# Hybrid attention and HGRN2 block: value tiles turned in 32x32 blocks at eviction instead of by TensorE transposes

## The chip, the cores and the metric

One Trainium2 chip, of which the kernel uses one core. The metric is the device time of one execution in microseconds (us); where several executions are timed, their median. Inputs and output are float32, batch 1, 1024 tokens, model width 1024.

The engines are named as the profile names them: PE (TensorE matmul; PEld is its weight load), DVE (VectorE), ACT (ScalarE), POOL (GpSimd) and SP (SyncE, which here issues most of the DMAs). SBUF is the on-chip memory of 128 partitions, PSUM the memory that PE writes to, DRAM the memory off the core.

## The reference

One encoder block. Only the parts that touch "values" matter here:

```python
h = layer_norm(x, ln_in_g, ln_in_b)
proj = h @ w_in[l]                       # 1024 x 11776
aq, ak, av, hq, hf_fwd, hf_bwd, hi, hg, ga, gh = jnp.split(proj, split_idx, axis=-1)
att = dilated_attention(aq, ak, av, slopes)      # 3 groups (dilation 1, 4, 16) x 8 heads x 64
rec = hgrn2(hq, hf_fwd, hf_bwd, hi, hg, ...)     # 8 heads, 128 keys x 128 values
merged = sigmoid(ga) * (att @ w_att_up[l]) + sigmoid(gh) * (rec @ w_hgrn_up[l])
h = layer_norm(ALPHA * h + merged @ w_o[l], ...)
h = layer_norm(ALPHA * h + (silu(gate) * up) @ w_ffn_out[l], ...)

# attention inside one residue stream
o = jnp.einsum('nbhqk,nbkhd->nbqhd', p, vb) / l
# gated linear recurrence, chunk by chunk
o_intra = jnp.einsum('bhnij,bhnjv->bhniv', a, v)
u = jnp.einsum('bhnck,bhncv->bhnkv', k * jnp.exp(cum_last - cum), v)
```

The values are `av` (attention, 3 groups of 512 columns) and `hi` (recurrence, 1024 columns). In each of the three einsums the values are summed over tokens, so on PE they have to stand with tokens on the partitions. The projection leaves them the other way round, with its output columns on the partitions.

## The kernel before

The program has three phases. Phase 1 (to about 1173 us of the span) makes the whole projection and, woven into it, the attention and the recurrence; phase 2 the merge and `w_o`; phase 3 the feed-forward part. The change touches phase 1 alone.

**The projection, the main stream.** `stream` (L657) makes the 92 column tiles of `w_in`, 128 columns each, four at a time (two groups of two tiles). A pair of tiles is a 2x2 block product made with seven products instead of eight (`ORDER`, L628). Each product is 12 matmuls of 128x512 into one PSUM bank (`pj`): four slices of the inner dimension, and three float32r matmuls per slice (L273 to L275: high by high, high by low, low by high). Weights come in blocks of 128x512 (tile `wa`, issued by SP at L252), are split into `w_hi` (ACT, L215) and `w_lo` (POOL, L225), and three products lie between that split and its use. The sums of weight blocks that the scheme needs are made by DVE and POOL (L697 to L702).

**The evictions.** After four of the seven products a half tile (128 columns by 512 tokens) is complete, and an eviction function takes it out of the bank: `plain` (L564) for attention q, k, v and the recurrence's v; `tanhs` and `silu2` for the others. Where the scheme has a kept partial result (`add`), `plain` adds it in DVE (L573); where it has none (one half tile in four), ACT copies (L571). The half goes to a buffer `evh`, of which there are three, and from there SP stores it to a scratch tensor in DRAM (L574): `hg{h}v` for the recurrence's head h, `at{j}v{g}` for head pair j and group g. All scratch tensors are 128 columns (partitions) by 1024 tokens. For attention groups 1 and 2 the tokens are permuted on the way (`order_src`, `order_dst`), so that the tokens of one residue stream stand side by side. A bank that an eviction empties is written again three products later.

**The units, woven in.** When a unit's columns are stored, it begins: eight units of `hgrn_side` (one head each) and four pairs of `att_far` (groups 1 and 2) and `att_near` (group 0). They are generators; each `yield` gives the number of products of the main stream that come before the next piece. Within what the yields allow, a scheduler orders each engine's instructions. A unit fetches its tensors from scratch (`fetch`, L773) into slots of SBUF. Values then are turned by `turned` (L784): eight PE transposes of 128x128 (L790, into two banks `sd`) and two ACT copies of 128x512 back to SBUF (L791). A recurrence head does that once (tile `hv`), a pair of attention heads three times (tile `v` of group 1, `vt` of group 2, `v` of group 0). Group 2 needs its tokens in yet another order first, which POOL makes with two copies (L899).

What comes next in a unit: in the recurrence the transposes of the keys (L1197), their copies (L1198) and the state products (L1213), which use `hv`; in `att_far` the transposes of the probabilities (L911, L919) and the products with the values (L942 to L951); in `att_near` L1072 and L1088.

Of the kernel before, what the change touches and what calls it, by code (L numbers as in the profile page):

```python
# [10 lines left out]
F32 = mybir.dt.float32  # L11
# [9 lines left out]
T = 1024  # L21
KT = D // 128
HALF = 512
# [8 lines left out]
HQ, HF, HB, HI, HG = 4608, 5632, 6656, 7680, 8704  # L32
# [47 lines left out]
class Block:  # L80
    evac_ahead = 1000

    def __init__(self, ctx, tc, x, ln_in_g, ln_in_b, w_in, hgrn_lb, hgrn_norm_g, w_att_up, w_hgrn_up,
                 w_o, ln1_g, ln1_b, w_ffn_in, w_ffn_out, ln2_g, ln2_b, tabs, out, dbg=None):
        self.tc, self.nc, self.ctx = tc, tc.nc, ctx
        self.x = x[0]
        self.ln = {"in": (ln_in_g, ln_in_b), "1": (ln1_g[0], ln1_b[0]), "2": (ln2_g[0], ln2_b[0])}
        self.w_in, self.lbw, self.ng = w_in[0], hgrn_lb, hgrn_norm_g[0]
        self.wa, self.wr, self.wo = w_att_up[0], w_hgrn_up[0], w_o[0]
        self.wfi, self.wfo, self.tabs, self.out = w_ffn_in[0], w_ffn_out[0], tabs, out[0]  # L90
        self.dbg = dbg or {}
# [12 lines left out]
        def scratch(name, n):  # L104
            if name in self.dbg:
                return [self.dbg[name][i] for i in range(n)]
            return [dram.tile([128, 1024], F32, name=f"{name}{i}") for i in range(n)]

        self.att_d = scratch("att", 4)
        self.rec_d = scratch("rec", 8)  # L110
        self.tg_d = scratch("tg", 16)
        self.n1_d = scratch("n1", 8)
        self.ahs_d = scratch("ahs", 8)
        self.hg_d = [{n: dram.tile([128, T], F32, name=f"hg{h}{n}") for n in ("t0", "t1", "q", "v", "g")}
                     for h in range(8)]
        self.at_d = [{(k, g): dram.tile([128, T], F32, name=f"at{j}{k}{g}") for k in "qkv" for g in range(3)}
                     for j in range(4)]
        self.w_d = [dram.tile([32, 128], F32, name=f"wd{j}") for j in range(4)]
        self.td = [dram.tile([128, 4, HALF], F32, name=f"td{i}") for i in range(3)]
        self.gd = {p: dram.tile([128, NF // 2, HALF], F32, name=f"gd{p}") for p in range(1, 8)}  # L120
        self.consts()
# [442 lines left out]
    def plain(self, dst, g=0, kind="v"):  # L564
# [10 lines left out]

        return evac

    def tanhs(self, dst):
        nc = self.nc

        def evac(l, ps, add):
            t = self.evh()
            if add is not None:
                self.left(nc.vector.tensor_add(t, add, ps))  # L584
            nc.scalar.activation(t, ps if add is None else t, AF.Tanh, scale=0.5)
            nc.sync.dma_start(dst[:, HALF * l:HALF * (l + 1)], t)

        return evac
# [16 lines left out]
    def tiles(self):  # L605


        out, units = [], []
        for i in range(4):
            for h in (2 * i, 2 * i + 1):  # L610
                d = self.hg_d[h]
                for n, col, f in (("t0", HF, self.tanhs), ("t1", HB, self.tanhs), ("q", HQ, self.silu2),
                                  ("v", HI, self.plain), ("g", HG, self.silu2)):
                    out.append((col + 128 * h, f(d[n], len(out) % 2) if n in "qg" else f(d[n])))
                units.append((len(out), h, self.hgrn_pre, self.hgrn_side))
            for g in (1, 2, 0):
                for kind, off in (("q", AQ), ("k", AK), ("v", AV)):
                    out.append((off + 512 * g + 128 * i, self.plain(self.at_d[i][kind, g], g, kind)))
                if g == 2:
                    units.append((len(out), i, self.att_pre, self.att_far))  # L620
            units.append((len(out), i, self.near_pre, self.att_near))
        for i in range(16):
            out.append((GA + 128 * i, self.tanhs(self.tg_d[i])))
        return out, units
# [156 lines left out]
            self.nc.sync.dma_start(t, src)  # L781
        return t

    def turned(self, dst, cols):  # L784

        nc = self.nc
        for b in range(2):
            ps = self.ps_sd()
            for k in range(4):
                nc.tensor.transpose(ps[:, 128 * k:128 * (k + 1)], cols(4 * b + k), self.ident)  # L790
            nc.scalar.copy(dst[:, 4 * b:4 * b + 4, :], ps.rearrange("p (k d) -> p k d", k=4))  # L791
        return dst

    def att_small(self, n, w=8):
        return self.smt.tile([128, 2, w], F32, name=n, tag=n, bufs=1)
# [30 lines left out]
    def att_far(self, j, qk):  # L826


        nc, ident, HD, d = self.nc, self.ident, self.HD, self.at_d[j]
# [3 lines left out]
        q, k = qk  # L833
# [19 lines left out]
        for r in range(4):  # L853
# [5 lines left out]
            for hd, ps in enumerate(pss):  # L859
                for h in range(2):  # L860
                    s, c = slice(192 * h, 192 * h + 192), 2 * r + h
                    self.ttr(P1(r, hd)[:, s], ps[:, s], bias[hd][:, s], M1[:, hd, c:c + 1])
            if r % 2:
                yield 2
        v1, v2 = self.fetch(0, "v1", d["v", 1], True), self.fetch(1, "v2", d["v", 2])
        k2 = k2.rearrange("p (h r i m) -> p r i h m", h=2, r=4, i=4)
        for b in range(2):
            pss = [self.ps_sd().rearrange("p (t c) -> p t c", t=4) for _ in range(2)]
            for jj in range(4):
                r, h = divmod(4 * b + jj, 2)  # L870
# [13 lines left out]
        for r in range(4):  # L884
            for hd in range(2):
                s1, _, s2, _ = self.FAR[2 * r + hd]
                for h in range(2):
                    c = 2 * r + h
# [5 lines left out]
                        nc.scalar.activation(v, v, AF.Exp, bias=N12[:, hd, c:c + 1], scale=QSCALE,  # L894
                                             accum_out=l[:, hd, c:c + 1])
        nc.vector.tensor_add(L12, L12, LB)
        V2 = self.slot(6, "vt2", (8, 128))
        for h in range(2):
            nc.gpsimd.tensor_copy(V2.rearrange("p k (i h m) -> p (k i) h m", i=2, h=2)[:, :, h],  # L899
                                  v2[:, HALF * h:HALF * (h + 1)].rearrange("p (k m) -> p k m", m=32))  # L900
        yield 2
        V1 = self.turned(v1.rearrange("p (k d) -> p k d", k=8), lambda kt: v1[:, 128 * kt:128 * kt + 128])
        self.turned(V2, lambda kt: V2[:, kt, :])
        yield 2


        def turn1(r):
            for hd in range(2):
# [74 lines left out]
    def att_near(self, j, pre):  # L983
# [3 lines left out]
        OL, N12, L12 = self.far  # L987
        q, k, bias = pre
        M0, N0, L0 = (self.att_small(n) for n in ("M0", "N0", "L0"))
        v = self.fetch(0, "v0", d["v", 0])  # L990
        yield 1
        P = []

# [7 lines left out]
        for b in range(4):  # L1001
# [272 lines left out]

    def hgrn_side(self, h, st):
        nc = self.nc
        v = self.fetch(5, "hv", self.hg_d[h]["v"])
        st["fa"] = self.slot(6, "fa")
        steps = [self.hgrn_dir(h, d, st) for d in range(2)]
        for _ in range(2):  # L1280
            for z in steps:
                next(z)
                yield 1
        vT = self.turned(v.rearrange("p (k d) -> p k d", k=8), lambda c: v[:, 128 * c:128 * c + 128])
        k0 = self.hgrn_keys(st, 0)
        for z in steps:
            next(z)
# [755 lines left out]
```

## Time and profile before

| | us |
|---|---|
| three timed executions | 2032.02, 2033.93, 2038.81 (median 2033.93) |
| the profiled execution, its own time | 2036.54 |
| its span in the profile | 2034.7 |
| granted TensorE clock, mean | 0.998 |
| busy: PE, DVE, POOL, ACT | 2003.3, 1312.7, 1013.0, 957.6 |
| DMA: bytes moved, share of 16 engines (SP's queue) | 301 MB, 42.8% |

The profile is one execution. Its page has the busy time of each engine, slices of the span, the DMA queues, the chain that ended last, and groups of equal instructions with their releasers. Beside it, answers of the trace are used: a stretch of the timeline, the instructions of one line or one tile, busy times by windows of 50 us, and who waited for whom. Matmuls overlap in their pipeline, so what one costs is read from start to start and not from its duration. A column of three numbers such as 270/272/273 is shortest/median/longest in ns.

### The profile page before, as it was taken

The page shows a single profiled execution, that of the slowest core. Times are in us where ns is not written, and L with a number is a line of the kernel's source. Part 1 is how long each engine was busy: PE and PEld are TensorE (multiplying, and loading weights), DVE is VectorE, ACT ScalarE, POOL GpSimd, SP SyncE. Part 2 cuts the span into 40 slices and gives each one's busy share as a digit, 9 for nine tenths or more (in the row PEclk, how much of TensorE's full clock was granted, in tenths as well). Part 3 has the DMA queues.
Part 4 walks back from the last instruction along what each step waited for, and adds up shares of the span by engine and source line. Part 5 has one row for each costly group of instructions (what it writes and reads, how often), then busy time and mean ns, then how long its engine had stood idle before and what let it go on. Part 6 is the DMA issues. An engine that isn't in the chain of part 4 may idle for free. (4 is left out here: it accounts for less than half of the span.)

```text
span 2034.7 us, 30875 instructions
## 1 busy us (share of the span) xinstructions
PE 2003.3 (98%) x10942; PEld 1661.3 (82%) x10942; DVE 1312.7 (65%) x2065; ACT 957.6 (47%) x1976; POOL 1013.0 (50%) x882
## 2 busy tenths in 40 slices
PE   7999999999999999999999999999999999999998
PEld 5788888788888888888888888888788888888886
DVE  7876544875458843778444226557776776767788
ACT  6654455554556535655365423244433333344541
POOL 6556653576436663466645662243765665630000
PEclk9999999999999999999999999999999999999999
DMA  5444543345343453443535377444444443347533
GB/s 160 129 132 138 170 127 109 138 149 162 122 150 126 133 173 107 141 136 124 178 99 177 125 255 235 147 145 139 139 136 140 135 140 130 128 169 288 166 97 126
DMA packets 275900, 301.16 MB, mean 148 GB/s; under 512 B 14433, under 2 KB 207906, under 8 KB 275746
## 3 DMA queue, kind: packets, MB, share of 16 engines
q1 hardware_dynamic: 269248, 277.93, 42.8%
q10 hardware_dynamic: 6498, 21.27, 2.7%
q8 instruction: 86, 1.41, 0.3%
q14 instruction: 68, 0.56, 0.1%
HBM read 204.96 MB, written 94.18 MB: 147 GB/s over the span
## 5 line engine op out<-in xcount | busy, mean ns | idle before, releaser
L225 POOL TENSOR_TENSOR w_lo<-wa,w_hi 128x512 fp32r<-128x512 f32 x272 | 363.8, 1347 | 286.8 <-ACT w_hi L215 253.4
L215 ACT CAST w_hi<-wa 128x512 fp32r<-128x512 f32 x272 | 168.5, 620 | 249.7 <-PE pj L274 143.9
L225 POOL TENSOR_TENSOR w_lo<-wsum,w_hi 128x512 fp32r<-128x512 f32 x88 | 127.9, 1464 | 111.1 <-PE sd L275 60.7
L225 POOL TENSOR_TENSOR w_lo<-f_raw,w_hi 128x512 fp32r<-128x512 f32 x66 | 100.9, 1536 | 51.8 <-ACT w_hi L215 50.7
L211 POOL TENSOR_TENSOR mv<-mv,mhalf 128x1 f32<-128x1 f32 x16 | 12.7, 792 | 221.7 <-DVE mv L210 221.6
L215 ACT CAST w_hi<-wsum 128x512 fp32r<-128x512 f32 x88 | 54.6, 621 | 116.7 <-PE sd L274 108.8
L215 ACT CAST gwsum<-a_raw 128x512 fp32r<-128x512 f32 (+1 forms) x78 | 48.2, 618 | 112.2 <-PE pj L274 53.6
L273 PE MATMUL pj<-xt1hi,w_hi 128*128 128x512 f32 x252 | 99.8, 396 | 0.0
L275 PE MATMUL pj<-xt1hi,w_lo 128*128 128x512 f32 x252 | 98.7, 392 | 0.0
L274 PE MATMUL pj<-xt1lo,w_hi 128*128 128x512 f32 x252 | 98.4, 391 | 0.0
L699 POOL TENSOR_TENSOR wa<-wa,wa 128x512 f32<-128x512 f32 x46 | 66.6, 1449 | 55.2 <-DVE wa L698 52.1
L225 POOL TENSOR_TENSOR w_lo<-ws,w_hi 128x512 fp32r<-128x512 f32 x46 | 63.7, 1387 | 57.5 <-ACT w_hi L215 47.3
L584 DVE TENSOR_TENSOR evh<-wkeep,pj 128x512 f32<-128x512 f32 x45 | 30.8, 684 | 93.4 <-PE pj L275 50.6
L573 DVE TENSOR_TENSOR evh<-wkeep,pj 128x512 f32<-128x512 f32 x66 | 57.9, 884 | 37.4 <-PE pj L275 28.7
L727 ACT COPY wkeep<-pj 128x512 f32<-128x512 f32 x136 | 79.5, 586 | 0.1
L273 PE MATMUL pj<-xt2hi,w_hi 128*128 128x512 f32 x192 | 76.5, 399 | 2.0 <-ACT w_hi L215 2.0
L275 PE MATMUL pj<-xt2hi,w_lo 128*128 128x512 f32 x192 | 76.5, 399 | 1.0 <-POOL w_lo L225 0.8
L274 PE MATMUL pj<-xt2lo,w_hi 128*128 128x512 f32 x192 | 76.3, 397 | 0.6 <-DVE xt2lo L405 0.6
L225 DVE TENSOR_TENSOR gwkeep<-a_raw,gwsum 128x512 fp32r<-128x512 f32 (+1 forms) x78 | 53.1, 680 | 36.1 <-ACT gwsum L215 33.2
L273 PE MATMUL pj<-xt4hi,w_hi 128*128 128x512 f32 x192 | 76.3, 397 | 0.0
L273 PE MATMUL pj<-xb11hi,w_hi 128*128 128x512 f32 x192 | 75.9, 398 | 0.3 <-DVE evh L600 0.3
L274 PE MATMUL pj<-xb11lo,w_hi 128*128 128x512 f32 x192 | 75.7, 395 | 0.0
(448 smaller groups left out, 6564.9 us busy)
## 6 DMA issues: line engine op xcount, KB each, us to landing
wa<-in_w_in_dram SPq DMA_DIRECT2D x184, 256.0 KB, 3.5
f_raw<-in_w_ffn_in_dram SPq DMA_DIRECT2D x44, 512.0 KB, 4.1
a_raw<-gd SPq DMA_DIRECT2D x30, 512.0 KB, 3.7
gd<-fc SPq DMA_DIRECT2D x44, 256.0 KB, 2.0
gd<-fs SPq DMA_DIRECT2D x33, 256.0 KB, 2.1
tg<-evh SPq DMA_DIRECT2D x32, 256.0 KB, 2.5
tg<-tg SPq DMA_DIRECT2D x16, 512.0 KB, 5.8
y<-ahs SPq DMA_DIRECT2D x16, 512.0 KB, 6.6
```

The lines of the kernel that those rows point to most:

```text
L211: nc.gpsimd.tensor_tensor(mv[:, 2:3], mv[:, 2:3], self.mhalf[:, 0:1], OP.pow)
L215: ins = nc.scalar.copy(hi, src) if eng_hi == "act" else nc.vector.tensor_copy(hi, src)
L225: ins = e.tensor_sub(lo, src, hi.bitcast(F32))
L273: nc.tensor.matmul(ps, whi, xhi, start=first, stop=False, **kw)
L274: nc.tensor.matmul(ps, whi, xlo, start=False, stop=False, **kw)
L275: self.product = nc.tensor.matmul(ps, wlo, xhi, start=False, stop=last, **kw).ins.name
L573: self.left(nc.vector.tensor_tensor(o, self.order_src(add, g, kind), s, OP.add))
L584: self.left(nc.vector.tensor_add(t, add, ps))
L699: nc.gpsimd.tensor_sub(a["a21"], a["a22"], a["a11"])
L727: nc.scalar.copy(t, ps)
```

## The change

Values are turned where they leave the projection, and never on PE.

- The eviction of a value half is now `rows`. It adds the kept part in DVE where there is one (plain order, no permutation), then one DVE instruction, `transpose`, turns each 32x32 block of the 128x512 half in place; without a kept part the transpose reads the bank itself. A block then has tokens on its 32 partitions, but the blocks still stand where they stood. The store puts them in their places: four DMAs, one for each group of 32 columns, write 32 x 16 pieces of 32 floats (128 bytes) into a scratch tensor that has 1024 rows (tokens) of 128 floats.
- The units fetch the values as rows with `fetch_rows`: tokens come to the partitions by the address pattern of the load. Group 0 and the recurrence take one DMA, group 1 two, group 2 eight (32 partitions each); the order by residue streams, which `order_src` and POOL's copies made before, lies in those patterns.
- `turned` is gone, with its transposes and copies, and POOL's copies for group 2. The yields are unchanged. `plain` stays for q and k.

```diff
-        self.hg_d = [{n: dram.tile([128, T], F32, name=f"hg{h}{n}") for n in ("t0", "t1", "q", "v", "g")}
+        self.hg_d = [{n: dram.tile([128, T], F32, name=f"hg{h}{n}") for n in ("t0", "t1", "q", "g")}
...
+        for h in range(8):
+            self.hg_d[h]["v"] = dram.tile([T, 128], F32, name=f"hg{h}v")
+        for j in range(4):
+            self.at_d[j].update({("v", g): dram.tile([T, 128], F32, name=f"at{j}v{g}") for g in range(3)})
...
+    def rows(self, dst):
+        nc = self.nc
+
+        def evac(l, ps, add):
+            t = self.evh()
+            if add is not None:
+                self.left(nc.vector.tensor_add(t, add, ps))
+            nc.vector.transpose(t, ps if add is None else t)
+            for a in range(4):
+                s = slice(32 * a, 32 * a + 32)
+                nc.sync.dma_start(dst[HALF * l:HALF * (l + 1), s].rearrange("(b i) j -> i b j", i=32),
+                                  t[s, :].rearrange("i (b j) -> i b j", j=32))
+
+        return evac
...
-                                  ("v", HI, self.plain), ("g", HG, self.silu2)):
+                                  ("v", HI, self.rows), ("g", HG, self.silu2)):
...
-                    out.append((off + 512 * g + 128 * i, self.plain(self.at_d[i][kind, g], g, kind)))
+                    dst = self.at_d[i][kind, g]
+                    out.append((off + 512 * g + 128 * i, self.rows(dst) if kind == "v" else self.plain(dst, g, kind)))
...
-    def turned(self, dst, cols):
-
-        nc = self.nc
-        for b in range(2):
-            ps = self.ps_sd()
-            for k in range(4):
-                nc.tensor.transpose(ps[:, 128 * k:128 * (k + 1)], cols(4 * b + k), self.ident)
-            nc.scalar.copy(dst[:, 4 * b:4 * b + 4, :], ps.rearrange("p (k d) -> p k d", k=4))
-        return dst
+    def fetch_rows(self, n, name, src, g=0):
+
+        t = self.slot(n, name, (8, 128))
+        if g == 0:
+            self.nc.sync.dma_start(t, src.rearrange("(k p) d -> p k d", p=128))
+        elif g == 1:
+            z = src.rearrange("(h x r) d -> h x r d", h=2, r=4)
+            for h in range(2):
+                self.nc.sync.dma_start(t.rearrange("p (r h) d -> p r h d", h=2)[:, :, h], z[h])
+        else:
+            z = src.rearrange("(h m e i r) d -> i h e m r d", h=2, e=2, i=2, r=4)
+            for i in range(2):
+                for h in range(2):
+                    for e in range(2):
+                        p = 64 * i + 32 * h
+                        self.nc.sync.dma_start(t.rearrange("p (r e) d -> p r e d", e=2)[p:p + 32, :, e], z[i, h, e])
+        return t
...
-        v1, v2 = self.fetch(0, "v1", d["v", 1], True), self.fetch(1, "v2", d["v", 2])
+        V1, V2 = self.fetch_rows(0, "v1", d["v", 1], 1), self.fetch_rows(1, "v2", d["v", 2], 2)
...
-        V2 = self.slot(6, "vt2", (8, 128))
-        for h in range(2):
-            nc.gpsimd.tensor_copy(V2.rearrange("p k (i h m) -> p (k i) h m", i=2, h=2)[:, :, h],
-                                  v2[:, HALF * h:HALF * (h + 1)].rearrange("p (k m) -> p k m", m=32))
         yield 2
-        V1 = self.turned(v1.rearrange("p (k d) -> p k d", k=8), lambda kt: v1[:, 128 * kt:128 * kt + 128])
-        self.turned(V2, lambda kt: V2[:, kt, :])
         yield 2
...
-        v = self.fetch(0, "v0", d["v", 0])
+        V = self.fetch_rows(0, "v0", d["v", 0])
...
-        V = self.turned(v.rearrange("p (k d) -> p k d", k=8), lambda kt: v[:, 128 * kt:128 * kt + 128])
...
-        v = self.fetch(5, "hv", self.hg_d[h]["v"])
+        vT = self.fetch_rows(5, "hv", self.hg_d[h]["v"])
...
-        vT = self.turned(v.rearrange("p (k d) -> p k d", k=8), lambda c: v[:, 128 * c:128 * c + 128])
```

The order in which the instructions stand shows what becomes of three places. Line numbers of the change are some lines higher than those of before (L573 is L588, L273 is L277, L911 is L932, L697 is L717).

PE, first pair of attention heads, before: the transposes of the values (L790) between two products of the main stream (`pj<-...`).

```order
L275 MATMUL pj<-xb21hi,w_lo 128x512
L790 MATMUL sd<-tabs_sb,v_2778 128x128 x8
L273 MATMUL pj<-xt2hi,w_hi 128x512
L274 MATMUL pj<-xt2lo,w_hi 128x512
L275 MATMUL pj<-xt2hi,w_lo 128x512
L273 MATMUL pj<-xt2hi,w_hi 128x512
L790 MATMUL sd<-tabs_sb,vt_2860 128x128 x8
L274 MATMUL pj<-xt2lo,w_hi 128x512
L275 MATMUL pj<-xt2hi,w_lo 128x512
```

The same engine with the change, two products later, where the transposes of the probabilities (L932, `pf`; L911 before) now begin.

```order
L277 MATMUL pj<-xt2hi,w_hi 128x512
L278 MATMUL pj<-xt2lo,w_hi 128x512
L279 MATMUL pj<-xt2hi,w_lo 128x512
L932 MATMUL sd<-tabs_sb,pf 128x128 x12
L277 MATMUL pj<-xt1hi,w_hi 128x512
L278 MATMUL pj<-xt1lo,w_hi 128x512
```

The sixteen transposes are gone, the main stream's matmuls follow each other there, and the probabilities' transposes stand 24 main matmuls behind the place of the first L790; before they stood 62 behind it. Over the program PE has 160 instructions less and returns from woven-in work to the main stream 132 times instead of 160.

DVE, first head of the recurrence, before: the eviction of the first value half (L573) between that of a forget gate (L584) and sums of weight blocks (L697, L698); the second half is ACT's and not in this order.

```order
L584 TENSOR_TENSOR evh<-wkeep,pj 128x512
L404 TENSOR_TENSOR xt4lo<-v_249,xt4hi 128x512
L573 TENSOR_TENSOR evh<-wkeep,pj 128x512
L1111 TENSOR_TENSOR lbm<-vc_260 128x16
L584 TENSOR_TENSOR evh<-wkeep,sd 128x512
L1112 RECIPROCAL lbm<-lbm 128x16
L697 TENSOR_TENSOR ws_913<-wa_768,wa_911 128x512
```

With the change the same stretch, and the rows of the second half.

```order
L603 TENSOR_TENSOR evh<-wkeep,pj 128x512
L408 TENSOR_TENSOR xt4lo<-v_249,xt4hi 128x512
L588 TENSOR_TENSOR evh<-wkeep,pj 128x512
L1130 TENSOR_TENSOR lbm<-vc_260 128x16
L603 TENSOR_TENSOR evh<-wkeep,sd 128x512
L589 STREAM_TRANSPOSE evh<-evh 128x512
L1131 RECIPROCAL lbm<-lbm 128x16
L717 TENSOR_TENSOR ws_913<-wa_768,wa_911 128x512
...
L722 TENSOR_TENSOR wa_841<-wa_841,wa_670 128x512
L589 STREAM_TRANSPOSE evh<-pj 128x512
```

The transpose of the first half stands two rows behind its addition, ahead of the sums; that of the second half takes the bank itself and stands behind the last of those sums (L722). In the whole program there are 40 such transposes, 30 from `evh` and 10 from a bank.

SP, around the fetch of the first attention pair's values, before: stores of halves (`<-evh`), fetches of values (`v`) and queries (`q`), loads of weights (`wa`).

```order
L574 DMA at0v_161<-evh 128x512
L574 DMA at0k_158<-evh 128x512
L586 DMA hg2t_125<-evh 128x512
L778 DMA v_2778<-at0v_162 128x4x128 x2
L781 DMA v_2781<-at0v_163 128x1024
L781 DMA q_3210<-at0q_155 128x1024
L574 DMA hg2v<-evh 128x512
L252 DMA wa_2761<-in_w_in_dram 128x4x128
```

With the change:

```order
L592 DMA at0v_179<-evh 32x16x32 x4
L578 DMA at0k_150<-evh 128x512
L605 DMA hg2t_123<-evh 128x512
L812 DMA v_2792<-at0v_180 128x4x128 x2
L819 DMA v_2795<-at0v_181 32x4x128 x8
L256 DMA wa_2775<-in_w_in_dram 128x4x128
L256 DMA wa_2885<-in_w_in_dram 128x4x128
L605 DMA hg2t_124<-evh 128x512
L592 DMA hg2v<-evh 32x16x32 x4
```

A store of a value half is four DMAs, the fetch of group 2 eight. The fetch of the near unit's queries (`q_3210`) has moved back: its slot now holds group 2's values until `att_far` has used them, and it stands with that of the keys.

More of the change, by code (lines that the diff above doesn't have):

```diff
@@ L113, in __init__ @@
         self.ahs_d = scratch("ahs", 8)
-        self.hg_d = [{n: dram.tile([128, T], F32, name=f"hg{h}{n}") for n in ("t0", "t1", "q", "v", "g")}
+        self.hg_d = [{n: dram.tile([128, T], F32, name=f"hg{h}{n}") for n in ("t0", "t1", "q", "g")}
                      for h in range(8)]
-        self.at_d = [{(k, g): dram.tile([128, T], F32, name=f"at{j}{k}{g}") for k in "qkv" for g in range(3)}
+        self.at_d = [{(k, g): dram.tile([128, T], F32, name=f"at{j}{k}{g}") for k in "qk" for g in range(3)}
                      for j in range(4)]
+        for h in range(8):
+            self.hg_d[h]["v"] = dram.tile([T, 128], F32, name=f"hg{h}v")
+        for j in range(4):
+            self.at_d[j].update({("v", g): dram.tile([T, 128], F32, name=f"at{j}v{g}") for g in range(3)})
         self.w_d = [dram.tile([32, 128], F32, name=f"wd{j}") for j in range(4)]
```

## The prediction

> **What bounds the kernel now.** I read the page's busy times first, then who waited for whom on PE in the stretch of phase 1 behind its start (110 to 1175 us).
>
> ```profile
> span 2034.7 us, 30875 instructions
> PE 2003.3 (98%) x10942; PEld 1661.3 (82%) x10942; DVE 1312.7 (65%) x2065; ACT 957.6 (47%) x1976; POOL 1013.0 (50%) x882
> PEclk9999999999999999999999999999999999999999
> ...
> PE sd L1213 <- ACT hkT L1198: 1.8, 3, 0.7
> PE sd L1197 <- POOL t L1183: 1.4, 2, 1.0
> PE pj L275 <- POOL w_lo L225: 1.0, 1, 1.0
> PE pj L273 <- DVE evh L600: 0.3, 1, 0.3
> ```
>
> PE is the bound: in 1065 us of phase 1 it waits 4.5 us in all, at the full clock. So time that leaves PE's queue leaves the program, as long as no new wait takes its place. What must hold for that is that work woven in isn't late at the end of phase 1:
>
> ```profile
> L1099 ACTq DMA_DIRECT2D att<-ol x4: 327/334/342, 358.9 to 1097.6; - x4
> L586 SPq DMA_DIRECT2D tg<-evh x32: 319/332/529, 994.8 to 1172.6; - x32
> ```
>
> The last unit stores its result at 1097.6 us, the main stream its last half at 1172.6. The units end 75 us early, so they set no end.
>
> **Part 1, the transposes on PE.** One group of eight in the timeline, the main stream around it (start, duration), and all of them by line:
>
> ```profile
> 276.30 0.40 PE L275 MATMUL pj<-xb21hi,w_lo 128*128 128x512 f32 x1
> 276.54 1.04 PE L790 MATMUL sd<-tabs_sb,v 128*128 128x128 f32 x8
> 277.33 0.47 PE L273 MATMUL pj<-xt2hi,w_hi 128*128 128x512 f32 x1
> 277.64 0.39 PE L274 MATMUL pj<-xt2lo,w_hi 128*128 128x512 f32 x1
> 277.87 0.40 PE L275 MATMUL pj<-xt2hi,w_lo 128*128 128x512 f32 x1
> ...
> L790 PE MATMUL sd<-tabs_sb,hv x64: 270/272/273, 126.6 to 932.7; 128*128 128x128 f32 x64
> L790 PE MATMUL sd<-tabs_sb,v x64: 270/272/273, 276.5 to 1068.8; 128*128 128x128 f32 x64
> L790 PE MATMUL sd<-tabs_sb,vt x32: 271/272/273, 278.3 to 1017.8; 128*128 128x128 f32 x32
> ```
>
> A main matmul follows the last by 0.23 us (277.64 to 277.87). Eight transposes push it on by 0.79 us (276.54 to 277.33), and the matmul behind them holds the array 0.31 us instead of 0.23. From 276.54 to 277.64 are 1.10 us, of which 0.23 would have passed anyway: 0.87 to 0.88 us for eight, 0.11 each. There are 64 + 64 + 32 = 160, twenty groups: 20 x 0.88 = **17.6 us** less on PE. The duration of 272 ns isn't the price, since they overlap.
>
> The Trainium skill (TensorE: Matmul & The Clock Gate, Part 4: PE-mode transpose) tells of about 275 ns for a transpose in one kernel's context; the trace agrees as to the duration, and the starts, 0.11 us apart, speak against taking it as a price. What it would give is the last rival.
>
> **Part 2, ACT and POOL.** ACT loses 40 copies of about 0.59 us and 10 evictions:
>
> ```profile
> L791 ACT COPY hv<-sd x16: 568/588/598, 127.3 to 934.8; 128x512 f32<-128x512 f32 x16
> L571 ACT COPY evh<-pj x22: 576/579/677, 90.6 to 984.6; 128x512 f32<-128x512 f32 x22
> ```
>
> Neither ACT nor POOL bounds, so the 23.6 + 5.8 us are worth nothing by themselves, nor are POOL's eight copies. But in a head of the recurrence the two copies of `hv` stood ahead of the copies of `hkT`, for which PE waited 1.8 us. Moved up by 1.2 us, these should end in time: **1.8 us** less; the wait is at most gone.
>
> **Part 3, DVE.** It gets 40 transposes of 128x512. No run shows one. The nearest rows:
>
> ```profile
> L584 DVE TENSOR_TENSOR evh<-wkeep,pj x45: 622/687/689, 78.4 to 1163.7; 128x512 f32<-128x512 f32 x45
> L573 DVE TENSOR_TENSOR evh<-wkeep,pj x66: 620/988/1146, 80.1 to 973.9; 128x512 f32<-128x512 f32 x66
> L1180 DVE RECIPROCAL qd<-fb x32: 1686/1740/1764, 126.4 to 953.3; 128x256 f32<-128x256 f32 x32
> ```
>
> One pass over a half costs 0.62 us at the least and, at the rate of the reciprocal (1.74 us for 256 columns), 3.48 us at the most. I take 0.69, the plain addition (L584), being nearest in shape and place: 27.6 us. Against it 12 value halves (groups 1 and 2, with a kept part) are no longer permuted in the addition: 0.99 to 0.69, 3.6 us less. DVE gets 24 us more (21 to 136). In most windows it idles a third of the time; it is dense in four:
>
> ```profile
> 50.00:100.00 50.00, 45.76 (x182) 34.51 (x182) 42.99 (x56) 31.59 (x55) 25.96 (x27) 0.95 0.40 127
> 350.00:400.00 50.00, 48.02 (x284) 39.99 (x283) 42.66 (x45) 24.46 (x49) 26.12 (x26) 1.00 0.44 150
> 600.00:650.00 50.00, 49.33 (x287) 41.43 (x285) 44.59 (x52) 27.27 (x60) 28.38 (x27) 1.00 0.45 146
> 850.00:900.00 50.00, 48.19 (x302) 39.82 (x301) 44.16 (x45) 28.17 (x63) 28.80 (x26) 1.00 0.41 137
> ...
> L574 SPq DMA_DIRECT2D hg3v<-evh x2: 319/366/414, 359.5 to 372.5; - x2
> L574 SPq DMA_DIRECT2D hg7v<-evh x2: 339/361/383, 871.7 to 882.8; - x2
> ```
>
> (The third number is DVE's busy time in 50 us.) About two value halves fall into each, as those of heads 3 and 7 do: 8 x 0.69 = 5.5 us. There DVE has 5 to 7 us of idle time left, and a bank has three products, 3 x 12 x 0.227 = 8.2 us, until it is written again. Where the addition is first and the bank is free before the transpose, that cover holds; I let 2 us of the 5.5 through to PE (0 to 5.5): **+2 us**.
>
> **Part 4, stores and queue.** 40 stores become 160 on SP, each of the same 256 KB now in 2048 pieces of 128 bytes. The nearest rows for small pieces:
>
> ```profile
> q1 hardware_dynamic: 269248, 277.93, 42.8%
> ...
> wa<-in_w_in_dram SPq DMA_DIRECT2D x184, 256.0 KB, 3.5
> ...
> DMA to landing us min/median/max: 2.0/2.4/6.9
> L574 SPq DMA_DIRECT2D at0v<-evh x6: 319/329/457, 179.4 to 255.4; - x6
> ```
>
> SP's queue took 0.428 x 2034.7 = 871 us of all 16 engines for 269248 packets: 52 ns a packet on one engine, of 1032 bytes in the mean. Priced by bytes, the new stores cost what they do now; priced by packets, 2048 x 52 / 16 = 6.6 us a half. I take the weight load as nearest: also 256 KB in pieces (512 bytes), it lands in 3.5 us, against 2.4 for an eviction. Then a buffer `evh` is held for 0.7 + 0.7 + 4 x 0.33 + 3.5 = 6.2 us (9.3 at the dear end). Evictions come at best one per product, 2.7 us, and there are three buffers: 8.2 us. At 6.2 nothing waits; at 9.3 DVE stands for 1.1 us, with additions and sums of weights queued behind it and 8.2 us to the bank's next use. So **0**. On SP the stores wait for the transpose, 0.7 us longer than now, with weight loads behind them; 148 more issues of 0.33 us (the eight of group 2's fetch among them) are 49 us of some 900. The split of a weight block stands three products ahead of its use, another 8.2 us. The Trainium skill (DMA: Bandwidth & Descriptors, Specifications) speaks against this part: transfers under 512 bytes fall below line rate, with a read-modify-write. No run here shows such a store; it argues for the dear end, which changes the sum by nothing.
>
> **Part 5, fetches and moved steps.**
>
> ```profile
> L781 SPq DMA_DIRECT2D hv<-hg0v x1: 497/497/497, 99.9 to 99.9; - x1
> L1213 PE MATMUL sd<-hv,hkT x224: 270/275/377, 136.6 to 954.0; 128*128 128x128 f32 x112
> 278.43 0.55 ACT L894 ACTIVATE pf<-pf,NL 128x320 f32<-128x320 f32 x1
> ```
>
> Values as rows are now needed at L1213 instead of L790: issued at 99.9 and used at 136.6, 36 us for a landing of some 5. No price. In `att_far` the probabilities' transposes come 24 main matmuls behind 276.54, at 282.0 us; the eighth exponential, the last that the first twelve need, ends at 279.0. The cover is 3 us; if it failed, four pairs would pay what is missing. The near queries' fetch moves to that of the keys, which already had the same wait. No price.
>
> **Sum.** 2036.5 - 17.6 - 1.8 + 2 = **2019.1 us** for an execution like the profiled one. That one lay 2.6 us above the median of 2033.9, so the median goes to **2016.5 us**, 0.9% less.
>
> **Rivals.**
> - *DVE takes over in its dense windows.* Its idle time there is made of waits for PE that it cannot use ahead, so all that is added reaches PE and the chain through `qd`, `t` and `hkT` too: 5.5 us twice instead of 2 once, 9 us more, 2025.5. For it: PE's busy time (first number) falls short of 50 in just these windows. Against it: 8.2 us until a bank is needed. 12%.
> - *No change.* The removed transposes filled time in which PE would have waited for a unit, so the waits grow by what they shrink: 2031 to 2034. Against it: between the eight and the next woven piece stand main matmuls that wait for nothing. 8%.
> - *Slower: a dear transpose.* At the reciprocal's rate (3.48 us) the eight halves in the dense windows bring 28 us that find 5 to 7 us of idle time per window, already used in part, and if all of it reaches PE: 2033.9 - 19.4 + 28 = 2042.5. It decides from (19.4 + 6.1) / 8 = 3.2 us a transpose. For it: nothing here shows one. Against it: every pass over 128x512 in these rows but the reciprocal is under 1.2 us. 5%.
> - *Each transpose frees its whole duration:* 160 x 0.272 = 43.5 us, 1990. Starts 0.11 us apart speak against it; the Trainium skill's figure named in part 1 would give the same. 2%.
>
> **How the numbers follow.** Forecast 73%, 2010 to 2023 (waits that come and go in a rebuilt order, 6 us either way). The change does what it says: PE's list is 160 instructions shorter. The range 2009 to 2026 leaves out the second and third rival, the last, and some of the first: 2 in 10. About 0.3%, 6 us, is what a measurement can tell here: faster is the forecast, the last rival and most of the first, 85%; the same 10%; slower 5%.
>
> **What would show it.** In the profile after: no L790 and 160 matmuls less on PE, the main stream 0.23 us apart where they stood (part 1); L1213 no longer waiting for `hkT` (2); a transpose of about 0.7 us, and PE's waits for banks in the four windows under 2 us (3); the stores landing within 4 us, and no eviction waiting for a landing (4); no wait of L1213, L942 or L1088 for a fetch (5). Wrong would make it a transpose above 3 us, stores that land after 9, or weight splits that come late behind the stores.

## The result, and the profile after

| | before | with the change |
|---|---|---|
| median (five executions each) | 2035.31 us | **2016.65 us** |
| lowest, highest | 2032.02, 2038.81 | 2014.98, 2023.16 |
| ratio, 95% interval | | 0.9917 [0.9895, 0.994] |
| profiled execution, its own time | 2036.54 | 2021.5 |

Timed twice more, the change gave 0.9911 [0.9897, 0.9925] (`c_after`, 2017.02 us) and 0.991 [0.9894, 0.9926] (`y2_after_again`, 2018.61 us). It is 0.8 to 0.9% faster; 0.9% and 2016.5 us were forecast. (The ratios and intervals come from all executions of both kernels and are not quotients of the medians.)

The page of the kernel with the change: span, busy times of the engines, SP's queue.

```profile
span 2019.7 us, 30761 instructions
PE 1985.0 (98%) x10782; PEld 1644.0 (81%) x10782; DVE 1338.9 (66%) x2105; ACT 932.7 (46%) x1926; POOL 1008.1 (50%) x874
q1 hardware_dynamic: 362752, 277.94, 45.7%
```

PE has 160 matmuls and 18.3 us less of busy time, DVE 40 instructions and 26.2 us more, ACT 24.9 us less. The span is shorter by 15.0 us: not all that PE lost in work left the span.

The same kernel, who waited for whom on PE from 110 to 1160 us (in total, times, longest).

```profile
PE pj L279 <- POOL w_lo L229: 2.0, 1, 2.0
PE pj L277 <- DVE evh L619: 1.5, 1, 1.5
PE sd L1069 <- DVE WW L1066: 1.3, 3, 0.6
PE pj L277 <- DVE evh L589: 1.2, 1, 1.2
PE sd L1216 <- POOL t L1202: 1.0, 1, 1.0
```

The wait for `hkT` is gone, but the sum is 7.0 us where it was 4.5. Only one row, 1.2 us, names a transpose (L589); ahead of this stretch, at 90 us, stands one wait more for a transpose that reads a bank, 0.7 us. L619 is the eviction of a gate, and that for `w_lo` has grown from 1.0 to 2.0 us.

The transposes by line, the windows in which DVE is dense (behind the window's length the busy times of PE, PEld, DVE, ACT and POOL, then PE's granted clock), and the stores by what they move (KB each, median us to landing).

```profile
L589 DVE STREAM_TRANSPOSE evh<-evh x30: 648/700/715, 80.1 to 958.8; 128x512 f32<-128x512 f32 x30
L589 DVE STREAM_TRANSPOSE evh<-pj x10: 647/702/712, 89.4 to 972.3; 128x512 f32<-128x512 f32 x10
```

```profile
50.00:100.00 50.00, 46.40 (x188) 35.17 (x187) 42.22 (x56) 29.68 (x51) 24.94 (x23) 0.96 0.46 134
350.00:400.00 50.00, 47.13 (x276) 38.83 (x276) 44.18 (x51) 27.20 (x61) 27.38 (x26) 1.00 0.46 142
600.00:650.00 50.00, 49.01 (x303) 40.91 (x302) 44.70 (x51) 30.14 (x69) 32.22 (x31) 1.00 0.43 126
850.00:900.00 50.00, 47.97 (x315) 40.90 (x314) 40.05 (x46) 24.78 (x60) 33.40 (x31) 0.97 0.47 138
```

```profile
at0v<-evh SPq DMA_DIRECT2D x24, 64.0 KB, 2.0
at3v<-evh SPq DMA_DIRECT2D x24, 64.0 KB, 2.7
```

A transpose takes 0.70 us, from SBUF and from a bank alike. Two of them stand in each window, 1.4 us of busy time. DVE's busy time there was 42.7 to 44.6 us before and is 40.1 to 44.7 now (the windows are the same stretches of time, and the work in them stands some microseconds earlier now), and PE still falls short of 50. The two rows of stores land after 2.0 and 2.7 us in the median; others take longer (see part 4 below).

### The profile page after: what moved, and what is told of

The parts are those of the page before. It is cut to its first block, busy times and chain, and to the rows that moved or that the text cites. A ratio compares the mean times of both kernels' runs of the same rounds, so it can differ in the third digit from the quotient of the medians.

```text
span 2019.7 us, 30761 instructions
## 1 busy us (share of the span) xinstructions
PE 1985.0 (98%) x10782; PEld 1644.0 (81%) x10782; DVE 1338.9 (66%) x2105; ACT 932.7 (46%) x1926; POOL 1008.1 (50%) x874
## 5 line engine op out<-in xcount | busy, mean ns | idle before, releaser
L277 PE MATMUL pj<-xt1hi,w_hi 128*128 128x512 f32 x252 | 100.0, 397 | 0.7 <-DVE evh L589 0.7
L603 DVE TENSOR_TENSOR evh<-wkeep,pj 128x512 f32<-128x512 f32 x45 | 30.8, 685 | 89.0 <-PE pj L279 52.6
L277 PE MATMUL pj<-xt2hi,w_hi 128*128 128x512 f32 x192 | 76.6, 400 | 2.0 <-ACT w_hi L219 2.0
L277 PE MATMUL pj<-xb11hi,w_hi 128*128 128x512 f32 x192 | 75.9, 398 | 1.5 <-DVE evh L619 1.5
L277 PE MATMUL pj<-xt4hi,w_hi 128*128 128x512 f32 x192 | 75.9, 395 | 0.0
L279 PE MATMUL pj<-xb11hi,w_lo 128*128 128x512 f32 x192 | 75.4, 393 | 0.0
```

Source lines behind the costliest of these rows:

```text
L277: nc.tensor.matmul(ps, whi, xhi, start=first, stop=False, **kw)
L279: self.product = nc.tensor.matmul(ps, wlo, xhi, start=False, stop=last, **kw).ins.name
```

## The experiments

### What a transpose on PE is worth

`x1_pe_twice` is the kernel before with each of the 160 transposes made twice.

```diff
-            for k in range(4):
+            for k in (0, 1, 2, 3) * 2:
                 nc.tensor.transpose(ps[:, 128 * k:128 * (k + 1)], cols(4 * b + k), self.ident)
```

> The kernel before with each of the 160 value transposes on PE made twice into the same bank; copies on ACT and all else as they were. Theory A (a transpose costs PE its start-to-start distance of 0.11 us, and PE is the bound): 160 x 0.11 = 17.6 us longer than before, about 2053 us, ratio 1.0086. Rival B (a transpose costs its whole duration, 0.272 us): 43.5 us longer, ratio 1.021. Rival C (transposes fill time in which PE would wait for a unit): within 4 us of before, ratio below 1.002.

Measured: 2055.75 us, ratio 1.0087 [1.0066, 1.0107]. Its page, and the timeline of PE at the group of the prediction (start, duration):

```profile
PE 2020.9 (98%) x11102; PEld 1679.2 (82%) x11102; DVE 1320.2 (64%) x2065; ACT 958.7 (47%) x1976; POOL 1015.1 (49%) x882
```

```profile
278.24 1.91 PE L790 MATMUL sd<-tabs_sb,v 128*128 128x128 f32 x16
279.98 1.25 PE L790 MATMUL sd<-tabs_sb,vt 128*128 128x128 f32 x10
```

PE's busy time grows by 17.6 us for 160 transposes, and sixteen take 1.74 us from start to start. That is 0.11 us each, the term of part 1. The time grows by the ratio by 17.7 us, by the medians by 19.3; longer waits have a part in it (PE's from 110 us to 1160 us are 8.9 us, 4.5 before). With the whole duration the transposes would have cost 43.5 us.

### What the work on DVE costs

Two kernels change the number of transposes on DVE. `x2_no_turn` leaves the turning out, with a copy by ACT where the transpose read the bank (its values are not the reference's). `x3_turn_thrice` turns each half three times, which gives the same values as once.

```diff
x2_no_turn
-            nc.vector.transpose(t, ps if add is None else t)
+            if add is None:
+                nc.scalar.copy(t, ps)
x3_turn_thrice
             nc.vector.transpose(t, ps if add is None else t)
+            for _ in range(2):
+                nc.vector.transpose(t, t)
```

> The changed kernel without the 40 DVE transposes (a half without a kept part is copied by ACT, as before); it leaves out the turning of the blocks, so the values that the units read are not turned. Theory A (what DVE got is covered but for some 2 us): 0 to 3 us below the changed kernel, about 2015 us, ratio to before 0.990 to 0.992. Rival D (the DVE passes in the dense windows reach PE in full): 5.5 to 11 us below the changed kernel, ratio 0.986 to 0.989.

> The changed kernel with three DVE transposes for each value half instead of one (80 more of 0.70 us, 56 us of DVE, 11 us of it in the four dense windows). Theory A (about a third of what is added in the dense windows reaches PE): 3 to 5 us above the changed kernel, about 2021 us, ratio to before 0.993. Rival D (all of it reaches PE there): 11 us or more above the changed kernel, ratio 0.997 or more.

Measured: x2 2015.73 us, ratio 0.99 [0.9886, 0.9915]; x3 2024.08 us, ratio 0.9939 [0.9924, 0.9953]. Without any turning the kernel is within 0.2% of the change (2 to 4 us), inside the intervals, and from the 300th matmul of the main stream to the end its profile takes 1912.1 us, the change's three profiles 1910.3 to 1913.1: no price of the forty transposes can be seen. Eighty more cost some 0.3% (0.9939 against 0.9911 to 0.9917 for the change, 4.5 to 6 us), a little more than expected. Here are the longest of PE's waits of x2, and of x3, in the same stretch.

```profile
PE pj L277 <- DVE evh L620: 3.1, 1, 3.1
PE pj L279 <- POOL w_lo L229: 1.8, 1, 1.8
PE sd L1217 <- POOL t L1203: 1.0, 1, 1.0
PE sd L1233 <- ACT hkT L1218: 0.8, 1, 0.8
```

```profile
PE pj L277 <- DVE evh L621: 3.2, 2, 2.5
PE pj L279 <- POOL w_lo L229: 2.0, 1, 2.0
```

With no transpose in the kernel, PE waits longer for the same gate's eviction (L620 there, L619 in the change, L600 before) than with them, 3.1 us against 1.5. So these waits aren't made by the transposes. What makes them shows in DVE's timeline of the changed kernel:

```profile
361.51 0.67 DVE L617 TENSOR_TENSOR pj<-wkeep,pj 128x512 f32<-128x512 f32 x1
362.09 1.74 DVE L1199 RECIPROCAL qd<-fa 128x256 f32<-128x256 f32 x1
363.75 2.05 DVE L1181 TENSOR_TENSOR_SCAN fb<-fb,d 128x528 f32<-128x528 f32 x1
365.72 0.66 DVE L619 SCALAR_TENSOR_TENSOR evh<-evh,pj 128x512 f32<-128x512 f32 x1
...
372.71 1.74 DVE L1199 RECIPROCAL qd<-fa 128x256 f32<-128x256 f32 x1
374.37 0.65 DVE L589 STREAM_TRANSPOSE evh<-pj 128x512 f32<-128x512 f32 x1
```

The gate's last step (L619) stands behind a reciprocal and a scan of head 3, without a pause between them. DVE before the change, the first and the last of the same four:

```profile
366.71 0.67 DVE L598 TENSOR_TENSOR pj<-wkeep,pj 128x512 f32<-128x512 f32 x1
...
370.93 0.66 DVE L600 SCALAR_TENSOR_TENSOR evh<-evh,pj 128x512 f32<-128x512 f32 x1
```

They follow each other in the same 4.2 us, and PE waited 0.3 us for them (the row with L600). PE now has less to do in this place and is there earlier, so it waits 1.5. What it no longer does are eight of the transposes, which stood directly ahead of this wait. PE before, and then with the change:

```profile
370.30 1.04 PE L790 MATMUL sd<-tabs_sb,hv 128*128 128x128 f32 x8
371.64 0.50 PE L273 MATMUL pj<-xb11hi,w_hi 128*128 128x512 f32 x1 [0.30 <-DVE evh L600]
```

```profile
366.44 0.50 PE L277 MATMUL pj<-xb11hi,w_hi 128*128 128x512 f32 x1 [1.55 <-DVE evh L619]
```

Here the 0.88 us that eight transposes cost came back as waiting in full. In the other profiles of the two kernels this wait is 0.7 us (before, `y1_before_again`) and 2.4 and 1.5 us (change, `c_after` and `y2_after_again`). The transpose from the bank waits its turn too, behind a reciprocal, rather than being long: PE waits 1.2 us for an instruction of 0.65 (in `c_after`, where the wait for the gate is 2.4 us, not at all). In such a place DVE sets the pace, and what PE saves comes back as waiting.

In `x5_act_first` ACT copies the bank and DVE turns the copy, so that no bank waits for a transpose.

```diff
-            nc.vector.transpose(t, ps if add is None else t)
+            if add is None:
+                nc.scalar.copy(t, ps)
+            nc.vector.transpose(t, t)
```

> The changed kernel, but a half without a kept part is copied from the bank by ACT as before, and DVE turns it in the buffer like the others. Theory A (the bank is what PE waits for where DVE is dense; the profile of the changed kernel has 1.2 us of such a wait behind the transpose): 1 to 2 us below the changed kernel on this chip. Rival F (the bank's reader makes no difference): within 1 us of it.

Measured: 2015.37 us, ratio 0.9903 [0.9889, 0.9917], against 2017.02 and 0.9911 of the change on the same chip. The intervals overlap, and from the 300th matmul of the main stream to the end its profile takes 1911.6 us, that of `c_after` 1911.3. No gain is shown: the wait for L589 is gone, but so it is in `c_after`, and that for the gate is 2.0 us. The wait for a bank at 90 us is 0.3 us where the change has 0.7.

### What small pieces cost

`x4_plain_store` stores a half with one DMA, 2 KB per partition. The placing of the blocks is left out, so its values are not the reference's.

```diff
-            for a in range(4):
-                s = slice(32 * a, 32 * a + 32)
-                nc.sync.dma_start(dst[HALF * l:HALF * (l + 1), s].rearrange("(b i) j -> i b j", i=32),
-                                  t[s, :].rearrange("i (b j) -> i b j", j=32))
+            nc.sync.dma_start(dst[HALF * l:HALF * (l + 1), :].rearrange("(p b) d -> p (b d)", b=4), t)
```

> The changed kernel with one store per value half, 128 rows of 2 KB, instead of four with 2048 pieces of 128 bytes; it leaves out the placing of the blocks, so the values stand in another order. Theory A (the small pieces cost nothing): within 2 us of the changed kernel, ratio to before 0.991 to 0.993. Rival E (stores hold buffers and delay weights): 6 us or more below the changed kernel, ratio 0.989 or less.

Measured: 2014.86 us, ratio 0.9898 [0.9882, 0.9915], just under the range of theory A and 0.1 to 0.2% under the change, with overlapping intervals; from the 300th matmul to the end 1910.2 us, the change's three profiles 1910.3 to 1913.1. A price of the pieces, if there is one, is below what these runs can tell.

### The two parts apart, and a surplus that was none

`x6_attention_only` keeps the change for the attention and gives the recurrence its old eviction and `turned`; `x7_recurrence_only` the other way round. `c_after` is the change again.

```diff
x6_attention_only, against the change
-                                  ("v", HI, self.rows), ("g", HG, self.silu2)):
+                                  ("v", HI, self.plain), ("g", HG, self.silu2)):
...
-        vT = self.fetch_rows(5, "hv", self.hg_d[h]["v"])
+        v = self.fetch(5, "hv", self.hg_d[h]["v"])
...
+        vT = self.turned(v.rearrange("p (k d) -> p k d", k=8), lambda c: v[:, 128 * c:128 * c + 128])
```

> The changed kernel once more, on the chip on which the next three run. Every theory: ratio to before 0.990 to 0.994, about 17 us.

> The change for the attention values alone; the recurrence's values are turned on PE as before. Theory A: 96 transposes less on PE, 96 x 0.11 = 10.6 us, with about 1 us of DVE passes let through: 9.6 us below before, ratio 0.9953. Rival B (0.272 us each): 26 us, ratio 0.987. Rival G (the gain comes from the units' chains, the recurrence's above all, and not from PE's queue): less than 4 us, ratio above 0.998.

> The change for the recurrence's values alone; the attention's values are turned on PE as before. Theory A: 64 x 0.11 = 7.0 us less on PE and up to 1.8 us of waits for the copies of the keys, with about 1 us of DVE passes let through: 7 to 8 us below before, ratio 0.9963; together with the attention part the whole 17 us. Rival G (chains of the units): 12 us or more, ratio 0.994 or less.

Measured: x6 2019.35 us, ratio 0.9925 [0.9911, 0.9939]; x7 2028.4 us, 0.9965 [0.9952, 0.9978]; on that chip the kernel before had 2034.29 us. The recurrence's part is as expected by the ratio (0.9963), and 5.9 us by the medians. The attention's is worth 15 us where 9.6 was expected, a miss, and the parts sum to 21 us where both together give 17.

The surplus stands in the first 110 us (before, then x6; the first number in brackets counts PE's instructions, the number behind the fifth brackets is the clock):

```profile
0.00:110.00 110.00, 93.61 (x405) 72.30 (x406) 83.05 (x123) 68.70 (x112) 65.20 (x84) 0.97 0.48 151
```

```profile
0.00:110.00 110.00, 94.49 (x430) 74.19 (x431) 84.28 (x126) 70.93 (x116) 68.58 (x87) 1.00 0.52 162
```

x6 is 25 matmuls ahead, 5.6 us, though every engine's list is the same in both kernels up to the first store of the attention's values, at 179 us. So nothing that the edit changes in these lists explains it. In both, PE waits 1.99 us for the same weight split; here are PE's first matmul behind it and windows of 2 us from there, before and then x6:

```profile
47.22 0.50 PE L273 MATMUL pj<-xt2hi,w_hi 128*128 128x512 f32 x1 [1.99 <-ACT w_hi L215]
```

```profile
48.00:50.00 2.00, 2.00 (x6) 0.98 (x5) 2.00 (x3) 2.00 (x4) 2.00 (x2) 0.67 0.00 0
50.00:52.00 2.00, 1.44 (x4) 1.06 (x4) 2.00 (x4) 0.79 (x2) 0.15 (x1) 0.50 0.00 0
52.00:54.00 2.00, 2.00 (x7) 1.51 (x7) 1.27 (x2) 0.00 (x0) 0.00 (x0) 0.50 0.35 131
54.00:56.00 2.00, 2.00 (x8) 1.69 (x7) 1.41 (x2) 0.65 (x2) 0.00 (x0) 0.63 0.00 0
```

```profile
45.84 0.49 PE L277 MATMUL pj<-xt2hi,w_hi 128*128 128x512 f32 x1 [1.99 <-ACT w_hi L219]
```

```profile
50.00:52.00 2.00, 2.00 (x12) 1.65 (x11) 2.00 (x4) 0.00 (x0) 0.00 (x0) 1.00 0.35 131
52.00:54.00 2.00, 2.00 (x10) 1.65 (x9) 1.86 (x3) 1.41 (x3) 0.00 (x0) 1.00 0.00 0
```

Before, the clock granted falls to half behind the wait; in x6 it doesn't. The trace of before has the clock at half for 6.8 us there, which can make at most 3.4 of the 5.6 us; another 1.1 us of lead x6 has from the main stream's first matmul on (16.0 us, 17.1 before). Four more runs asked whether that belongs to a kernel or to an execution, and whether the parts add up once the start is taken out.

> A second profile of the kernel before. Theory S (the start varies from execution to execution: up to about 107 us every engine's list is the same in this kernel and in the one with the attention's part alone, and yet that one's profile was 5.6 us ahead there, with 25 more matmuls in the first 110 us): the profile differs from the first one by the start, by 0 to 6 us, and from the 300th matmul of the main stream to the end of the span it takes 1927 us again, within 1.5 us. Rival T (the start belongs to the kernel): the 300th matmul starts at 107.6 us again, within 1 us.

> S: median 2015 to 2018; the start (300th matmul of the main stream) anywhere from 101 to 107 us, and from there to the end 1911 to 1913 us, 14 to 16 us less than before. T: the start at 104 to 107 us.

> The attention's values as rows, the recurrence as before. S: from the 300th matmul to the end 1915 us, 12 us less than before (96 transposes x 0.11 = 10.6, and little else), and the median 12 us under that of before plus or minus what the starts differ by, so between 2018 and 2024. T: the start at 102 us again and the median 15 us under that of before.

> The recurrence's values as rows, the attention as before. S: from the 300th matmul to the end 1923 us, 4 us less than before (64 transposes x 0.11 = 7.0, less the new waits for banks of the transposed halves, 1.9 and 1.5 us), median 2025 to 2031. The two parts then add up to 16 us, what both have together. T: the two parts sum to 21 us in the medians again.

The medians: y1 2036.5 us, 1.0003 [0.9991, 1.0015] against other executions of the same kernel; y2 2018.61, 0.991; y3 2019.03, 0.9926 [0.9912, 0.994]; y4 2030.32, 0.9976 [0.9965, 0.9986]. From the profiles, the start of the 300th matmul of the main stream, and the time from there to the end of the span:

| us | start | from there to the end | less than before |
|---|---|---|---|
| before, y1 | 107.6, 106.2 | 1927.1, 1928.1 | |
| change: first profile, c_after, y2 | 106.6, 103.8, 106.8 | 1913.1, 1911.3, 1910.3 | 16.0 |
| attention alone: x6, y3 | 102.0, 102.2 | 1915.2, 1914.5 | 12.8 |
| recurrence alone: x7, y4 | 103.4, 109.0 | 1922.9, 1922.4 | 5.0 |

(The last column takes the means.) The same kernel starts at 103.4 once and at 109.0 another time, so the start varies by execution; how it goes with the clock is told at the end. In x6 and y3 it was short both times, as T had it, and their executions lie mostly low (four of y3's six between 2018.5 and 2019.2, the others 2022.4 and 2024.7); why it is short there more often isn't settled. T's other sign didn't come: in the medians the two parts were 14.8 and 3.5 us the second time, 18.2 in all, and both together 15.2. S missed by little in y2, whose median lies 0.6 us above its range and whose later stretch 0.7 us below.

Behind the start each kernel repeats within 3 us, and the parts sum to 17.8 us against 16.0: they add up within what the profiles differ by. So the first 21 us were in part a matter of the starts. The start isn't free of the edit either: head 0's value halves are evicted in it, at 80 and 89 us. But from the 200th to the 300th matmul pass 25.6 and 25.5 us before, 26.0, 26.7 and 25.9 with the change, and 26.3 in x6, whose lists there are those of before, so what the table leaves out is about 1 us at most.

## Why the prediction was right, step by step

- **Part 1** holds. 17.6 us was forecast; PE's busy time fell by 18.3, and x1 put 17.6 on it.
- **Part 2**: the wait of L1213 (now L1232) for `hkT`, 1.8 us, is gone as forecast. The reason given, ACT's copies ahead of it, isn't shown: in x7, whose recurrence is that of the change, ACT makes no copy of `hv` either, and 0.8 us of the wait are there, and in x6, where ACT still makes them, it is 1.1.
- **Part 3** has nearly the right size and partly the wrong cause. A transpose takes 0.70 us (forecast 0.69), and DVE has 26.2 us more (24). The waits for banks in the dense windows are 1.5 + 1.2 us and 0.7 at 90 us, 3.4 us, of which 0.3 were there before; forecast were 2, and the sign "under 2 us" wasn't met. And the step said that the transposes let them through. x2 shows the larger one without a transpose: DVE's chain in head 3 kept its pace and PE came early. For `w_lo` it is the same, in head 7. POOL's splits around its wait, with the change and before, and the eight transposes that PE made between the two before:

```profile
843.23 1.71 POOL L229 TENSOR_TENSOR w_lo<-wa,w_hi 128x512 fp32r<-128x512 f32 x1 [4.79 <-ACT w_hi L219]
...
854.16 1.26 POOL L229 TENSOR_TENSOR w_lo<-wa,w_hi 128x512 fp32r<-128x512 f32 x1
```

```profile
855.67 1.71 POOL L225 TENSOR_TENSOR w_lo<-wa,w_hi 128x512 fp32r<-128x512 f32 x1 [4.53 <-ACT w_hi L215]
...
866.60 1.27 POOL L225 TENSOR_TENSOR w_lo<-wa,w_hi 128x512 fp32r<-128x512 f32 x1
```

```profile
857.25 0.71 PE L790 MATMUL sd<-tabs_sb,hv 128*128 128x128 f32 x5
858.26 0.38 PE L790 MATMUL sd<-tabs_sb,hv 128*128 128x128 f32 x2
863.50 0.27 PE L790 MATMUL sd<-tabs_sb,hv 128*128 128x128 f32 x1
```

  From one to the other POOL takes 10.93 us both times, with the head's products in between, and PE's wait goes from 1.0 to 2.0 us (1.8 in x2). That is the first profile of each; in the change's other two the wait is 1.3 us, in y1 1.2, so this place is less sure than the gate's. So the rival "no change" was right at one of the twenty groups, in this profile at two, and not in general.
- What the sum had no term for: that second wait (1.0 us more in this profile), 1.3 us for `WW` (L1069), whose cause stays open, and the half clock behind the 2.0 us wait, told below, 1.6 us.
- **Part 4** holds in its price, not in all its signs. x4 finds no price. Of the 160 stores the trace has the landing of 80: the median is 2.1 us, under the 3.5 taken, but 8 take over 4 us, up to 6.7. The pieces aren't shown to make that: before, 6 of 21 such stores took over 4, up to 6.4, and the first head's, 4.2 us in the median, take 4.6 in x4. One eviction, on ACT at 731.8 us, waits 0.3 us for a store, as one did before. Two splits of weights (3.9 us on ACT, 1.4 on POOL) are put down to such stores, and PE waits for neither. The dear end was 52 ns a packet on one engine. SP's queue has 93,504 packets more and took 0.457 x 2019.7 - 0.428 x 2034.7 = 52 us of 16 engines more, about 9 ns for each of them; by size, the trace has 13.5 ns for a packet of 128 bytes and 88.7 for one of 2 KB. So a half takes 2048 x 13.5 / 16 = 1.7 us of all engines where it took 128 x 88.7 / 16 = 0.7. An issue takes SP 0.49 us and not 0.33:

```profile
L592 SPq DMA_DIRECT2D at0v<-evh x24: 302/486/642, 181.0 to 255.3; - x24
```

  So the 49 us estimated for SP's issues were too few, without effect. The Trainium skill (DMA: Bandwidth & Descriptors, Specifications) puts transfers below 512 bytes under line rate. The packets agree (128 bytes in 13.5 ns, 2 KB in 88.7, so 9.5 bytes a ns against 23); the landing doesn't show it: 2.0 us for the 128-byte pieces at `at0v`, and 2.0 in x4, whose store of a half is one transfer.
- **Part 5** holds: no row of PE's waits names a fetch.

Added up for the profiled execution behind its start, from the 300th matmul to the 3600th at the end of the projection: 17.6 us less; waits of 7.0 instead of 4.5; 1.6 for the clock; 13.5 us less. Measured are 1001.4 - 987.0 = 14.4. In y2, whose waits are 6.0 us and none reaches 2, the same sum gives 16.1, measured 16.8. The forecast of 17.4 less was 1 to 3 us too much behind the start (16.0 in the mean of three profiles); that the medians came out so near it owes something to the starts. That the first median lies 0.15 us from the forecast is luck: the change's three medians are 2016.65 to 2018.61 us, those of the kernel before 2033.78 to 2036.5.

## What to carry to other kernels

Where one engine is busy to 98%, price an instruction by what it delays its neighbour, start to start, and count it once per place; for PE's busy time the forecast so made held to 0.7 us in 18. But look through the places one by one: where another engine's chain ends in step with the bound engine, time taken off the latter comes back as waiting, whatever the change adds elsewhere. And before a gain of a few microseconds is put down to an edit, compare two profiles over a stretch that the edit touches and over one that it doesn't.

## What the runs showed of the hardware

**Pauses of PE halve its clock for a while.** PE's timeline of the changed kernel, behind its longest wait of phase 1:

```profile
855.47 0.50 PE L279 MATMUL pj<-xb22hi,w_lo 128*128 128x512 f32 x1 [2.03 <-POOL w_lo L229]
855.81 0.39 PE L277 MATMUL pj<-xb22hi,w_hi 128*128 128x512 f32 x1
...
857.06 0.63 PE L278 MATMUL pj<-xb22lo,w_hi 128*128 128x512 f32 x1
857.49 0.63 PE L279 MATMUL pj<-xb22hi,w_lo 128*128 128x512 f32 x1
```

Matmuls that follow each other by 0.23 us do so by 0.43 from 856.6 to 859.6 us, seven times; with the steps at both ends 1.6 us are lost, beginning 1.2 us behind the wait. In the fourteen profiles PE waits over 1 us 44 times between 110 and 1990 us. The seven waits of 1.99 us or more are each followed by such a stretch; none of the 37 up to 1.89 us is. Near the start the length of the wait doesn't decide it. Eleven of the profiles have a wait of 1.985 to 1.997 us there: behind eight of these steps of 0.43 us follow, behind three (x2, x3, x6) none do, and in `c_after`, x4, x5 and x3 such steps follow waits of 1.25, 1.25, 1.37 and 1.52 us.

The clock's own records in the traces say more. In each of the thirteen profiles in which the clock falls before 1990 us, all its changes lie on a grid of 3.41 us, and where the grid stands differs from execution to execution. Cut at this grid, the fourteen traces have 8087 windows at the full clock up to 1990 us. In 15 of them PE is, by its records, idle for 1.79 us or more, all its pauses added, and half the clock follows each; in 10 it is idle for 1.62 to 1.77 us, and half the clock follows four; in the other 8062 it is 1.60 us at most, and half the clock follows none. So about half of a window is the bound, and a wait near 2 us that is shared by two windows can stay below it, which makes the executions of one kernel differ. Near the start the half clock lasts one window or two: where it lasts 6.8 us (six profiles) the 300th matmul starts at 106.2 to 109.0 us, where 3.4 us or not at all (seven) at 101.4 to 103.8, and in x3, which has 3.4 us of it at 84 us, at 105.5. The Trainium skill (TensorE: Matmul & The Clock Gate, HAM oscillation) warns of idle gaps of over some 3.4 us; here pauses of 1.8 us in sum within 3.41 were enough.

**Small pieces and transposes on DVE.** A 128-byte packet of the stores takes 13.5 ns of its DMA engine, as told above. The change's 40 transposes add 1338.9 - 1311.4 = 27.5 us to DVE's busy time against x2, which has none, 0.69 us each; in x3 80 more add 1379.6 - 1338.9 = 40.7 us, 0.51 each. DVE's busy time without the transposes differs between these profiles by up to 7 us (1315.6 in the change, 1308.2 in x3), so a transpose's share isn't known better than that.
